# Three pairs of column offsets, in turns, for the weight tiles of a decoder layer

## The chip, the cores and the metric

The kernel runs on one core of one Trainium2 chip. The metric is the device time of one execution in microseconds (us). TensorE (PE) multiplies: it loads a stationary block (LDWEIGHTS, shown as PEld) and streams moving columns past it. VectorE (DVE) and ScalarE (ACT) do elementwise work, GpSimd (POOL) a little of it, and SyncE (SP) issues most of the DMAs.

## The reference

One decoder layer on 256 tokens of width 1024, in float32. With 256 tokens there is one block of attention keys, so the attention is plain causal attention with eight heads.

```python
u = rms_norm(x, attn_pre_norm)
proj = u @ w_in                      # q, k, v, x_lru, g_lru, gate_attn, gate_lru
attn = moba_attention(partial_rope(q), partial_rope(k), v)
y_attn = attn @ w_branch_attn
xc = causal_depthwise_conv(x_lru, conv_w, conv_b)
hl = rg_lru(xc, w_rg_a, b_rg_a, w_rg_i, b_rg_i, lru_lambda)
y_lru = (hl * gelu(g_lru)) @ w_branch_lru
h = x + rms_norm((sigmoid(gate_attn) * y_attn + sigmoid(gate_lru) * y_lru) @ w_out, attn_post_norm)
m = square(relu(rms_norm(h, mlp_pre_norm) @ w_mlp_up)) @ w_mlp_down
out = h + rms_norm(m, mlp_post_norm)
```

## The kernel before

All weights come as 74 chunks of 128 partitions x 2048 float32 (1 MB each), in the order in which they are used. A product in float32 is made of three in the faster 32-bit type float32r: weights and activations are each split into a rounded part `hi` and a remainder `lo`, and `three` (lines 179 to 182) adds hi x hi, hi x lo and lo x hi into the same PSUM bank. `load` brings a chunk into one of three `wraw` buffers by a DMA on SP's queue. `split` (from line 102) writes `hi` on ScalarE (line 117; on VectorE for chunks 17 to 22, line 115) and `lo` on VectorE (line 118). `ahead` keeps four chunks loaded and two split ahead of the one in use.

The tiles `whi` and `wlo` have three buffers each, of 2048 + 64 columns of 4 bytes; `weight_tiles` (lines 96 to 100) takes 2048 columns of each, beginning at the column that the table `OFFSET` (line 45) gives for the chunk, 0 where it has no entry. All six buffers begin at multiples of 64 bytes, as the other large tiles do. The buffers are taken in turns, so up to chunk 39 the remainder of the chunk's number by 3 names the buffer; chunks 40 and 41 have tiles of their own, and from 42 on the turn is shifted by one.

The table names 48 chunks, those whose weights are the stationary operand: chunk 0 (`first_chunk`), 2, 4, 6, 8 to 15 (queries and keys), 16 and 17 (the two gates of the recurrence, lines 336 to 352), 18 to 29 (gates and GeLU branch), 30 to 37 (the two branch projections) and 44 to 57 (MLP up). Each is 48 matmuls of 256 columns (the tokens), for two blocks of 128 output features and eight blocks of input features; the order is `hi` with xh, `hi` with xl, `lo` with xh, so TensorE loads 48 stationary blocks of 128 x 128 per chunk, `hi` twice in a row and then `lo`. In the other chunks (values, output projection, the first two of MLP up, MLP down from 58 on) the weights are the moving operand, 512 columns at a time, and begin at column 0.

Between the feature chunks 18 to 29 stands an attention step each: for some heads the scores (lines 387 and 388), for others the transposes of the probabilities (line 405) and their product with the values (lines 411 and 412), all of them 32-bit matmuls in two passes. The last three steps have no scores left. Chunks 8 to 18 follow each other with nothing between them on TensorE, and so do 30 to 37 and 45 to 57. Ahead of 45 stand four transposes (line 613), ahead of 44 matmuls of 512 columns (lines 602 to 604).

The tile names in the rows: `xgh`, `xgl` are the two parts of the normalised input, `ath`, `atl`, `lrh`, `lrl` those of the branches, `u` both parts of the MLP's input, `rrh`, `rrl` those of its hidden layer.

Of the kernel before, what the change touches and what calls it, by code (L numbers as in the profile page):

```python
# [41 lines left out]

OFFSET = {c: (48, 16) for c in (*range(0, 8, 2), *range(8, 38), *range(44, 58))}


@with_exitstack
def hybrid_layer(ctx: ExitStack, tc: tile.TileContext, head_d, x_d, w_d, cst_d, gp_d, out_d):
# [45 lines left out]
    def weight_tiles(c):  # L95
        hi = whi_p.tile([P, 2048 + W_STEP], F32R, tag="whi", name=f"whi{c}")
        lo = wlo_p.tile([P, 2048 + W_STEP], F32R, tag="wlo", name=f"wlo{c}")
        h, l = OFFSET.get(c, (0, 0))
        return hi[:, h:h + 2048], lo[:, l:l + 2048]
# [637 lines left out]
```

## Time and profile before

| what | value |
|---|---|
| median of three runs | 442.46 us (442.3 to 617.95) |
| the profiled execution | 443.12 us, span 441.3 us |
| TensorE matmuls busy | 429.0 us, 97% |
| VectorE busy | 293.1 us, 66% |
| ScalarE busy | 239.7 us, 54% |
| granted TensorE clock, mean | 0.996 |
| DMA, mean | 189 GB/s |

The span goes from the first to the last instruction; 1.8 us of the execution lie around it. Matmuls overlap each other in the profile, and their ends are modelled, so a busy share near 100% says that TensorE always has something under way, and not at which rate; the rate is read from the starts.

### The profile page before, as it was taken

Reading aid. Unit: us, or ns where it says so; the run is one execution under the profiler, and the core shown is the slowest. Engines: PE = TensorE matmul, PEld = TensorE weight load, DVE = VectorE, ACT = ScalarE, POOL = GpSimd, SP = SyncE. Lnnn points to the kernel's source line nnn. Section 1 sums busy time; section 2 is a strip of 40 time slices with the busy share of each in tenths; the row PEclk is TensorE's granted clock in tenths of the full one; section 3 lists DMA queues with packets and bytes.
Section 4 is the critical chain, followed back from the end, with each engine's and each line's share of the span. In section 5 each row is a group of like instructions: output and inputs, shape, how many; then the busy total and the mean of one; then the engine's idle time right before and its main releaser. Section 6 shows DMA issues by size and latency. Waiting matters only on the chain.

```text
span 441.3 us, 7246 instructions
## 1 busy us (share of the span) xinstructions
PE 429.0 (97%) x3044; PEld 402.0 (91%) x3044; DVE 293.1 (66%) x353; ACT 239.7 (54%) x326; POOL 20.7 (5%) x48
## 2 busy tenths in 40 slices
PE   6989999999999999999999999999999999999994
PEld 6979999999999999999998879999999988888883
DVE  6749975779997666985688665666666644444424
ACT  7595753419977667553455566555555533333321
POOL 1000063202000000000000000000000000000000
PEclk9999999999999999999999999999999999999998
DMA  8968456655543455445567504555554555555202
GB/s 276 409 238 338 176 215 212 222 209 214 193 165 123 161 218 195 166 140 187 186 257 301 197 0 179 174 182 175 175 181 183 192 190 190 192 196 192 83 1 95
DMA packets 14576, 83.61 MB, mean 189 GB/s; under 512 B 1808, under 2 KB 2576, under 8 KB 5456
## 3 DMA queue, kind: packets, MB, share of 16 engines
q1 hardware_dynamic: 13520, 80.39, 50.7%
q0 software_dynamic: 736, 2.36, 1.6%
q8 instruction: 24, 0.39, 0.4%
q10 hardware_dynamic: 288, 0.39, 0.2%
q14 instruction: 8, 0.07, 0.0%
HBM read 81.04 MB, written 1.05 MB: 186 GB/s over the span
## 4 chain that ended last, share of the span: by engine, by line
PE 91%; DMA 5%; ACT 1%; DVE 1%; issue 0%; SPq 0%; DVEq 0%
PE mm L181 19%; PE mm L180 19%; PE mm L182 18%; PE acc L497 8%; PE acc L495 8%; PE acc L496 8%; DMA x_tok<-in_x_dram 2%; DMA wraw<-in_w_dram 1%; DMA xw_a<-in_head_dram 1%; PE up L604 1%; PE up L602 1%; PE v L233 1%; PE up L603 1%; PE v L234 1%; PE rg L181 1%; PE v L235 1%
## 5 line engine op out<-in xcount | busy, mean ns | idle before, releaser
L118 DVE TENSOR_TENSOR wlo<-wraw,whi 128x2048 fp32r<-128x2048 f32 (+2 forms) x78 | 163.6, 2099 | 88.3 <-ACT whi L117 87.9
L117 ACT CAST whi<-wraw 128x2048 fp32r<-128x2048 f32 (+2 forms) x72 | 125.2, 1739 | 95.8 <-PE acc L497 47.1
L180 PE MATMUL mm<-xgh,whi 128*128 128x256 f32 x384 | 107.7, 284 | 4.2 <-ACT xgh L171 4.2
L182 PE MATMUL mm<-xgh,wlo 128*128 128x256 f32 x384 | 106.6, 278 | 1.6 <-DVE wlo L118 1.6
L181 PE MATMUL mm<-xgl,whi 128*128 128x256 f32 x384 | 107.1, 280 | 0.0
L180 PEld LDWEIGHTS mm<-xgh,whi 128*128 128x128 f32 x384 | 72.2, 190 | 4.5 <-ACT xgh L171 4.2
L182 PEld LDWEIGHTS mm<-xgh,wlo 128*128 128x128 f32 x384 | 72.8, 189 | 1.8 <-DVE wlo L118 1.8
L181 PEld LDWEIGHTS mm<-xgl,whi 128*128 128x128 f32 x384 | 72.8, 189 | 0.5
L181 PE MATMUL mm<-u,whi 128*128 128x256 f32 x224 | 63.3, 283 | 0.0
L180 PE MATMUL mm<-u,whi 128*128 128x256 f32 x224 | 62.5, 279 | 0.0
L182 PE MATMUL mm<-u,wlo 128*128 128x256 f32 x224 | 62.4, 278 | 0.0
L497 PE MATMUL acc<-whi,rrl 128*128 128x512 f32 x128 | 49.8, 389 | 0.0
L496 PE MATMUL acc<-wlo,rrh 128*128 128x512 f32 x128 | 49.8, 389 | 0.0
L495 PE MATMUL acc<-whi,rrh 128*128 128x512 f32 x128 | 49.8, 389 | 0.0
L180 PEld LDWEIGHTS mm<-u,whi 128*128 128x128 f32 x224 | 42.1, 188 | 0.0
L182 PEld LDWEIGHTS mm<-u,wlo 128*128 128x128 f32 x224 | 42.0, 188 | 0.0
L181 PEld LDWEIGHTS mm<-u,whi 128*128 128x128 f32 x224 | 41.9, 187 | 0.0
L497 PEld LDWEIGHTS acc<-whi,rrl 128*128 128x128 f32 x128 | 24.0, 188 | 5.0
L496 PEld LDWEIGHTS acc<-wlo,rrh 128*128 128x128 f32 x128 | 24.0, 188 | 5.0
L495 PEld LDWEIGHTS acc<-whi,rrh 128*128 128x128 f32 x128 | 24.0, 188 | 4.9
L637 ACT CAST rrh<-rv 128x512 fp32r<-128x512 f32 x14 | 8.7, 621 | 34.6 <-DVE rv L636 34.6
L181 PE MATMUL mm<-atl,whi 128*128 128x256 f32 x64 | 18.1, 283 | 0.0
(197 smaller groups left out, 667.8 us busy)
## 6 DMA issues: line engine op xcount, KB each, us to landing
wraw<-in_w_dram SPq DMA_DIRECT2D x70, 1024.0 KB, 4.8
wraw<-in_w_dram SPq DMA_DIRECT2D x8, 256.0 KB, 6.1
xw_a<-in_head_dram SPq DMA_DIRECT2D x4, 256.0 KB, 4.3
wraw<-in_w_dram SPq DMA_DIRECT2D x2, 512.0 KB, 7.2
x_tok<-in_x_dram SPq DMA_DIRECT2D x1, 1024.0 KB, 10.5
gp<-in_gp_dram POOLq DMA_DIRECT2D x1, 1024.0 KB, 5.5
xw_b<-in_head_dram SPq DMA_DIRECT2D x3, 256.0 KB, 5.1
out_dram<-res ACTq DMA_DIRECT2D x2, 192.0 KB, 2.0
```

Of the source, the lines that this page charges most:

```text
L117: nc.scalar.copy(hi[:, k:(i + 1) * n], raw[:, k:(i + 1) * n])
L118: nc.vector.tensor_tensor(lo[:, s], raw[:, s], hi[:, s].bitcast(F32), ALU.subtract)
L180: nc.tensor.matmul(out, wh, xh, start=start, stop=False)
L181: nc.tensor.matmul(out, wh, xl, start=False, stop=False)
L182: nc.tensor.matmul(out, wl, xh, start=False, stop=stop)
L233: nc.tensor.matmul(banks[b], xgh[:, kb, s], hi[:, k, :], start=kb == 0, stop=False)
L234: nc.tensor.matmul(banks[b], xgh[:, kb, s], lo[:, k, :], start=False, stop=False)
L235: nc.tensor.matmul(banks[b], xgl[:, kb, s], hi[:, k, :], start=False, stop=kb == KB - 1)
L495: nc.tensor.matmul(out, xh[:, s], hi[:, hs], start=first, stop=False)
L496: nc.tensor.matmul(out, xh[:, s], lo[:, hs], start=False, stop=False)
L497: nc.tensor.matmul(out, xl[:, s], hi[:, hs], start=False, stop=last)
L637: nc.scalar.copy(hi, v)
```

## The change

The table of offsets has the same 48 chunks as before. Each had its `hi` tile begin at column 48 and its `lo` tile at column 16 of its buffer (192 and 64 bytes). Now the remainder of the chunk's number by 3 picks one of three pairs: 13 and 16 columns (52 and 64 bytes), 16 and 13, or 13 and 13.

```diff
-OFFSET = {c: (48, 16) for c in (*range(0, 8, 2), *range(8, 38), *range(44, 58))}
+OFFSET = {c: ((13, 16), (16, 13), (13, 13))[c % 3] for c in (*range(0, 8, 2), *range(8, 38), *range(44, 58))}
```

Sizes, buffers, the instructions of every engine and their order stay as they are; only the places differ from which `hi` and `lo` are read and to which they are written. The first pair has 17 of the 48 chunks, the second 15, the third 16.

## Rows read from the trace of the kernel before

**Rows 1.** The page's first line and its busy times (engine, us, share, instructions)

```profile
span 441.3 us, 7246 instructions
...
PE 429.0 (97%) x3044; PEld 402.0 (91%) x3044; DVE 293.1 (66%) x353; ACT 239.7 (54%) x326; POOL 20.7 (5%) x48
```

**Rows 2.** The page's chain that ended last, shares by engine, then by line

```profile
PE 91%; DMA 5%; ACT 1%; DVE 1%; issue 0%; SPq 0%; DVEq 0%
PE mm L181 19%; PE mm L180 19%; PE mm L182 18%; PE acc L497 8%; PE acc L495 8%; PE acc L496 8%; DMA x_tok<-in_x_dram 2%; DMA wraw<-in_w_dram 1%; DMA xw_a<-in_head_dram 1%; PE up L604 1%; PE up L602 1%; PE v L233 1%; PE up L603 1%; PE v L234 1%; PE rg L181 1%; PE v L235 1%
```

**Rows 3.** The page's costliest groups: busy us, mean ns of one, idle before

```profile
L180 PE MATMUL mm<-xgh,whi 128*128 128x256 f32 x384 | 107.7, 284 | 4.2 <-ACT xgh L171 4.2
...
L180 PEld LDWEIGHTS mm<-xgh,whi 128*128 128x128 f32 x384 | 72.2, 190 | 4.5 <-ACT xgh L171 4.2
```

**Rows 4.** Three stretches of feature chunks: us, engine busy (x instructions), clock, DMA

```profile
core 0: us, PE busy (x) PEld busy (x) DVE busy (x) ACT busy (x) POOL busy (x), PEclk, DMA share, GB/s
53.00:111.00 58.00, 58.00 (x514) 58.00 (x513) 44.90 (x44) 30.38 (x41) 18.11 (x38) 1.00 0.61 217
187.00:231.00 44.00, 44.00 (x373) 44.00 (x372) 32.04 (x28) 21.13 (x17) 0.00 (x0) 1.00 0.55 192
274.00:347.00 73.00, 73.00 (x617) 73.00 (x616) 46.55 (x39) 38.34 (x40) 0.00 (x0) 1.00 0.53 186
```

**Rows 5.** Windows of 3.6 us in chunks 19, 21, 22, 26, 27, 30, 44, 45

```profile
core 0: us, PE busy (x), PEclk, DMA share, GB/s
114.35:117.95 3.60, 3.60 (x34) 1.00 0.71 255
...
126.94:130.54 3.60, 3.60 (x32) 1.00 0.32 66
134.22:137.82 3.60, 3.60 (x34) 1.00 0.00 0
...
162.65:166.25 3.60, 3.60 (x34) 1.00 0.79 298
169.14:172.74 3.60, 3.60 (x32) 1.00 0.08 32
...
187.89:191.49 3.60, 3.60 (x32) 1.00 0.15 48
269.18:272.78 3.60, 3.60 (x34) 1.00 0.69 230
275.13:278.73 3.60, 3.60 (x32) 1.00 0.56 157
```

**Rows 6.** Timeline of TensorE (start, us, what), 512-column matmuls of the down projection

```profile
379.82 0.39 PE L496 MATMUL acc<-wlo,rrh 128*128 128x512 f32 x1
...
381.18 0.39 PE L496 MATMUL acc<-wlo,rrh 128*128 128x512 f32 x1
```

**Rows 7.** Timeline of TensorE, 32-bit matmuls of an attention step

```profile
124.23 0.49 PE L405 MATMUL pT<-ident,pr 128*128 128x128 f32 x3
124.56 0.39 PE L387 MATMUL s<-kT,qT 128*128 128x128 f32 x2
```

**Rows 8.** Groups by shape, then single lines: duration ns min/median/max

```profile
L118 DVE TENSOR_TENSOR wlo<-wraw,whi 128x2048 fp32r<-128x2048 f32 x68 | 155.7, 2290 | 86.2 <-ACT whi L117 86.1
...
L115 DVE CAST whi<-wraw 128x2048 fp32r<-128x2048 f32 x6 | 7.3, 1222 | 2.8 <-PE mm L181 2.6
...
L277 DVE SCALAR_TENSOR_TENSOR xc<-xlp,head,xc x24: 476/478/485, 33.7 to 57.8; 128x256 f32<-128x256 f32 x24
...
L272 DVE TENSOR_TENSOR xlp<-mm,rstd x3: 681/684/685, 40.5 to 48.7; 128x512 f32<-128x512 f32 x3
...
L325 DVE TENSOR_TENSOR qT<-mm,rstd x4: 682/692/692, 58.2 to 74.2; 128x512 f32<-128x512 f32 x4
```

**Rows 9.** Waits of TensorE: for whom, us in total, times, longest

```profile
PE mm L180 <- ACT xgh L171: 4.2, 1, 4.2
PE mm L182 <- DVE wlo L118: 1.6, 1, 1.6
```

## The prediction

> **What bounds the kernel now.** I read the page's busy shares first. TensorE's matmuls are busy for 429.0 of 441.3 us, VectorE for 293.1 and ScalarE for 239.7 [rows 1]. The chain of work that ended last says the same: 91% of it is TensorE, and the three lines of `three`, 180 to 182, hold 19 + 19 + 18 points of that [rows 2]. The view of waits of TensorE names two waits of 4.2 and 1.6 us for other engines and no more [rows 9]. So the time is a sum of distances from one matmul to the next, and a change of the operands' places counts only if it changes those distances (or makes VectorE or ScalarE so slow that TensorE has to wait).
>
> The duration of one matmul in the page (284 ns) is no distance: matmuls overlap, and so does the load of stationary data (190 ns) [rows 3]. The distance comes from a window without a break: matmuls counted in it, divided into the window plus one duration of 0.28 us, since the count takes in those still running at its left edge. From 53 to 111 us (chunks 8 to 18, the end of 18 left out) that is 58.28/514 = 113.4 ns; from 187 to 231 us (chunks 30 to 37) 44.28/373 = 118.7 ns; from 274 to 347 us (chunks 45 to 57) 73.28/617 = 118.8 ns [rows 4]. The granted clock is 1.00 in all three, the upper of its two levels, the instructions are the same, and no engine is waited for. So the same 48 matmuls of a feature chunk run in one of **two states**, which I call close and wide by their distances. They differ by 5.35 ns a matmul, 48 x 5.35 = 0.257 us a chunk.
>
> Which chunk is in which state is seen from equal windows of 3.6 us inside the chunks: 34 matmuls in the close state, 32 in the wide one [rows 5]. Of the 48 feature chunks (the two gate chunks counted in), chunk 0 runs piecewise behind its loads; close are 2, 4, 6, 8 to 20, 22 to 26 and 44, which makes 22; wide are 21, 27 to 37 and 45 to 57, 25 in all. The state is kept from chunk to chunk as long as nothing stands between them, and is chosen anew behind other matmuls: behind an attention step (chunks 19 to 30) or the transposes (chunk 45). Chunks 21 and 24 use the same weight buffers and the same moving tiles, and are in the wide and in the close state. So in this kernel the places alone do not decide the state; how the stream is entered does too.
>
> **The change, part by part.** No instruction is added, removed or moved on any engine; the bytes are the same. What changes is where a chunk's two weight tiles begin: 192 and 64 bytes into the buffer before, now 52 and 64, 64 and 52, or 52 and 52. Three things can follow.
>
> *The writes.* ScalarE writes `hi`, VectorE writes `lo` (2290 ns for one) and for chunks 17 to 22 `hi` too (1222 ns) [rows 8]. No row shows a write that begins off a multiple of 16 bytes. The nearest ones: reads of `xlp` at 1, 2 and 3 columns take 476 to 485 ns, all three alike, and the write of `xlp` at 4 columns takes 684 ns where the same shape to column 0 takes 692 [rows 8]. So I take nothing. If the double-rate copies of the four chunks with `hi` at 13 fell to 2290 ns, that would be 4 x 1.07 = 4.3 us, and VectorE is idle for 58 - 44.9 = 13.1 us of the busiest stretch [rows 4]. The cover is TensorE's own 5.4 us per chunk against some 44.9/58 x 5.4 = 4.2 us of VectorE; it is gone if a `lo` goes from 2.29 to 3.5 us.
>
> *The length of a load.* Two loads in three now begin 52 bytes into one of the 64-byte steps on which every tile began so far: 17 chunks x 32 + 15 x 16 + 16 x 48 = 1552 of the 2304 loads. No row shows such a load. The one on the grid is bounded by the passes of the 32-bit matmuls: three of `pT` start and give way to the next in 0.33 us, 110 ns each with a load of the same 128 x 128 in each [rows 7]. The close state's 113.4 ns is set by the moving data, since a matmul of twice the columns takes twice as long: six of 512 columns from 379.82 to 381.18 us, 226.7 ns each [rows 6]. That leaves the load a gap of 3.4 ns. The far ends of what a start off the grid costs are a gain (if it breaks the meeting that makes the wide state; that is the next part) and 190 - 113.4 = 77 ns, a load that overlaps nothing [rows 3]. The nearest row is the 110 ns of the same load on the grid, so I take a lengthening that stays within the gap: nothing in the close state, and in the wide one, where something beyond the stream is already on the path, the middle of 0 and 3.4 ns, 1.7 ns. [...]
>
> *The state.* The wide state costs 25 x 0.257 = 6.4 us now, and 22 chunks could still fall into it, 5.7 us. What the trace tells: entries behind scores of attention were close in seven of eight (chunks 19 to 26, 21 the exception), entries behind work without scores were wide in five of five (27, 28, 29, 30, 45), the one behind 512-column matmuls was close (44) [rows 5]. Two entries carry most of the wide time: chunk 30 hands its state on to 37 (8 chunks) and chunk 45 to 57 (13 chunks). I take the wide state for a meeting in time of the two streams that TensorE reads, and a start 52 bytes in shifts one against the other; so I expect entries to be drawn again, not all to one side. The likeliest single outcome is that one of the two long stretches turns to the close state: 10.5 chunks on average, -2.7 us. About 15 chunks remain wide, 15 x 48 x 1552/2304 = 485 loads off the grid at 1.7 ns, +0.8 us. Supply does not hold a gain back: the close stretch was fed at 217 GB/s, the long wide ones draw 192 and 186 [rows 4].
>
> **Sum.** -2.7 + 0.8 = -1.9 us. The profiled execution took 443.12 us (span 441.3, 1.8 around it), 0.66 over the median of 442.46; from the median, 440.6 us.
>
> **The rivals.**
> - *The offsets do not matter.* If TensorE's two reads do not meet, nothing changes: 442.5 us. For it: equal places gave both states. Against it: something makes equal instructions 5.35 ns longer while no engine is waited for. [...]
> - *The wide state goes.* A start off the grid keeps the reads from meeting in step: -6.4 us, 436.1 us. Against it: a third of the loads stays on the grid.
> - *Wide everywhere.* Both tiles now begin at nearly the same place of their grid, so what sets one wide sets the other wide: +5.7 us and 1552 loads at 0 to 3.4 ns, 448.1 to 453.4, 450.8 in the middle.
> - *The load off the grid becomes the bound*, the one that ends clearly on the other side. Every one of 1552 matmuls behind such a load waits for it. It passes 2% (8.9 us) when the load is 5.7 ns longer than the stream; at 10 ns it gives 458.0 us, at the 77 ns of a load that hides nowhere 562.0. For it: only 3.4 ns of gap. Against it: the load reads the same 512 bytes, and the reads at odd columns on VectorE cost nothing [rows 8].
> - *The stream itself gets quicker*, to the 110 ns of [rows 7]: 2304 x 3.4 = 7.8 us and the 6.4, 428.3 us. Against it: the same ratio holds for 512 columns, whose places are not touched.
>
> **How the numbers follow.** Forecast 0.42, its own range 437.5 to 444; no effect 0.15; wide state gone 0.15; wide everywhere 0.10; load as bound 0.13; quicker stream 0.05. A measurement of this kernel tells about 2% from no change, that is 433.6 and 451.3. Faster: 0.05. Slower: 0.13 and half of wide everywhere, 0.18. The rest, 0.77, is the same. The range goes from below the case without the wide state, 434.5, to 451.5, just past the middle of wide everywhere, which leaves out about 2 in 10.
>
> **What would show it.** The same windows: 53 to 111 us should again hold about 514 matmuls (a count near 490 means wide everywhere, less than that a load as the bound). The stretches of chunks 30 to 37 and 45 to 57 tell which state each is in, by 113.4 or 118.8 ns. Chunks of the three pairs can be told apart in turn: if the load matters, chunks whose number leaves 2 (both tiles off the grid) are slower than their neighbours by an equal amount everywhere. `lo` and the double-rate `hi` should keep 2290 and 1222 ns. I am wrong if a third distance appears, or if TensorE waits for a weight tile in the middle of the kernel.

## The result, and the profile after

The changed kernel takes 437.88 us (median of 437.08 to 438.56), 4.5 us less than the 442.38 us of before; the ratio to the runs of before is 0.9895, 95% interval 0.988 to 0.991. One execution of the kernel before took 617.95 us, a slow one, and without it that median would be 442.30. The change is faster, by about 1%, which is less than the 2% that the prediction takes as the border of "the same". The time lies in the range that the prediction states, and the gain is 2.4 times the 1.9 us that was forecast.

The page of the changed kernel, its first line and its busy times, to be held against [rows 1]:

```profile
span 436.8 us, 7246 instructions
...
PE 424.4 (97%) x3044; PEld 397.6 (91%) x3044; DVE 292.4 (67%) x353; ACT 238.5 (55%) x326; POOL 21.0 (5%) x48
```

The span is 4.5 us shorter, TensorE's busy time 4.6 us; the other engines did the same work. TensorE's waits for others are the two of [rows 9], word for word. The groups by shape show that the writes cost what they cost in [rows 8] (columns: busy us, mean ns of one, idle before and for whom):

```profile
L118 DVE TENSOR_TENSOR wlo<-wraw,whi 128x2048 fp32r<-128x2048 f32 x68 | 155.8, 2291 | 82.4 <-ACT whi L117 82.3
L117 ACT CAST whi<-wraw 128x2048 fp32r<-128x2048 f32 x62 | 118.3, 1908 | 88.5 <-PE acc L497 46.2 <-PE mm L181 32.3 <-issue 7.5
...
L115 DVE CAST whi<-wraw 128x2048 fp32r<-128x2048 f32 x6 | 7.3, 1224 | 2.7 <-PE mm L181 2.6
```

ScalarE's line before was this:

```profile
L117 ACT CAST whi<-wraw 128x2048 fp32r<-128x2048 f32 x62 | 118.1, 1905 | 93.6 <-PE acc L497 47.1 <-PE mm L181 38.8 <-issue 5.1
```

So the time has to be in the distances. Three windows stand for the three stretches with nothing between their chunks: 58 us in chunks 8 to 18, 42 us in 30 to 37, 68 us in 45 to 57 (the first 2.5 us of 45 left out). The distance is, as in the prediction, the window plus 0.28 us, divided by the matmuls in it. Before (columns: window, its length, TensorE busy and matmuls, clock, DMA share, GB/s):

```profile
52.70:110.70 58.00, 58.00 (x514) 1.00 0.61 217
186.70:228.70 42.00, 42.00 (x355) 1.00 0.53 189
275.80:343.80 68.00, 68.00 (x575) 1.00 0.52 183
```

The changed kernel:

```profile
53.20:111.20 58.00, 58.00 (x510) 1.00 0.61 215
187.30:229.30 42.00, 42.00 (x373) 1.00 0.55 198
274.70:342.70 68.00, 68.00 (x602) 1.00 0.52 186
```

Both long wide stretches are close: 42.28/373 = 113.4 ns where 119.1 stood, 68.28/602 = 113.4 where 118.7 stood. One matmul more or less in a window moves such a distance by 0.2 to 0.3 ns. The early stretch lost four matmuls. The windows of 3.6 us inside single chunks tell where (34 matmuls are the close state; compare [rows 5]); here chunks 2, 8, 9, 10, 28, 30, 44 and 45 of the changed kernel:

```profile
18.84:22.44 3.60, 3.60 (x32) 1.00 1.04 422
...
54.47:58.07 3.60, 3.60 (x32) 1.00 0.47 196
60.20:63.80 3.60, 3.60 (x33) 1.00 0.34 141
65.82:69.42 3.60, 3.60 (x34) 1.00 0.38 157
...
176.78:180.38 3.60, 3.60 (x33) 1.00 0.41 118
...
188.50:192.10 3.60, 3.60 (x34) 1.00 0.22 84
267.78:271.38 3.60, 3.60 (x32) 1.00 0.58 225
273.96:277.56 3.60, 3.60 (x34) 1.00 0.32 96
```

Seven chunks are wide: 2, 8 and 44 (pair 13 and 13) with 32, and 6, 9, 21 and 28 with 33. Chunk 8 is entered wide, 9 still is, 10 is not. Before, 2, 6, 8, 9 and 44 were close and 25 others wide; of those 25, 21 and 28 alone are left, and 23 became close. With the distances that the uniform runs below show, 119.9 ns for 13 and 13 and 117.7 for the others, the seven cost 3 x 48 x 6.5 + 4 x 48 x 4.3 ns = 0.9 + 0.8 = 1.8 us. Taken from the 6.4 us of the 25 that leaves 4.6 us, and the span is 4.5 us shorter. The whole change is accounted for by the distances.

The two long stretches are close from their first chunk on. The prediction counts chunk 30 as an entry, but nothing stands on TensorE between 29 and 30; in the kernel before the last matmul of 29 and the first of 30 are:

```profile
186.05 0.28 PE L182 MATMUL mm<-xgh,wlo 128*128 128x256 f32 x1
186.16 0.28 PE L180 MATMUL mm<-ath,whi 128*128 128x256 f32 x1
```

So the stretch runs from 29 to 37 and is entered at 29, behind an attention step. A window inside 29, before and then after, shows that it was entered wide and is now entered close:

```profile
182.18:185.78 3.60, 3.60 (x32) 1.00 0.24 36
```

```profile
183.06:186.66 3.60, 3.60 (x34) 1.00 0.19 25
```

The state is not there at once: 29 has 6 uneven distances before it is close, and 45 has 16, of 114 to 122 ns, inside the chunk and so with one pair. Neither stretch was thrown out of the wide state by a change of the pair. The one place where the changed kernel loses a steady wide state with nothing in between is from chunk 9 to 10. In no profiled run does a close chunk turn wide with nothing in between.

### The profile page after: what moved, and what is told of

Its sections match the earlier page's. It is cut to its first block, busy times and chain, and to the rows that moved or that the text cites. A ratio compares the mean times of both kernels' runs of the same rounds, so it can differ in the third digit from the quotient of the medians.

```text
span 436.8 us, 7246 instructions
## 1 busy us (share of the span) xinstructions
PE 424.4 (97%) x3044; PEld 397.6 (91%) x3044; DVE 292.4 (67%) x353; ACT 238.5 (55%) x326; POOL 21.0 (5%) x48
## 4 chain that ended last, share of the span: by engine, by line
PE 91%; DMA 5%; ACT 1%; DVE 1%; issue 0%; SPq 0%; DVEq 0%
PE mm L182 18%; PE mm L180 18%; PE mm L181 18%; PE acc L497 8%; PE acc L496 8%; PE acc L495 8%; DMA x_tok<-in_x_dram 3%; DMA wraw<-in_w_dram 1%; DMA xw_a<-in_head_dram 1%; PE up L602 1%; PE up L604 1%; PE rg L182 1%; PE v L234 1%; PE v L233 1%; PE up L603 1%; PE v L235 1%
## 5 line engine op out<-in xcount | busy, mean ns | idle before, releaser
L180 PE MATMUL mm<-u,whi 128*128 128x256 f32 x224 | 62.0, 277 | 0.0
L181 PE MATMUL mm<-u,whi 128*128 128x256 f32 x224 | 62.0, 277 | 0.0
L182 PE MATMUL mm<-lrh,wlo 128*128 128x256 f32 x64 | 17.7, 276 | 0.0
```

The lines of the kernel that those rows point to most:

```text
L180: nc.tensor.matmul(out, wh, xh, start=start, stop=False)
L181: nc.tensor.matmul(out, wh, xl, start=False, stop=False)
L182: nc.tensor.matmul(out, wl, xh, start=False, stop=stop)
```

## The experiments

Two theories were open after this. *Turns*: a steady wide state lives only as long as the stationary tiles keep their place from chunk to chunk, and the change of the pair ends it. *Off the grid*: a tile that begins 52 bytes in, off the 64-byte steps, cannot stay in the wide state. A third, *one pair*, gives all credit to 16 and 13, the pair of chunk 10.

All results in one table; the distances are those of the three windows, in ns, each from the profiled execution; times are medians. The kernel before, timed beside them, took 442.45 us in the first group of four (1 to 4), 442.61 in the second (5 to 8) and 442.46 in the third (9 to 11).

| run | 8 to 18 | 30 to 37 | 45 to 57 | us | ratio, 95% interval |
|---|---|---|---|---|---|
| before | 113.4 | 119.1 | 118.7 | 442.38 | |
| the change | 114.3 | 113.4 | 113.4 | 437.88 | 0.9895, 0.988 to 0.991 |
| 1: 13, 13 everywhere | 119.9 | 113.4 | 113.4 | 440.39 | 0.996, 0.9933 to 0.9987 |
| 2: 13, 16 everywhere | 117.7 | 117.8 | 113.4 | 440.83 | 0.9971, 0.9947 to 0.9995 |
| 3: 16, 13 everywhere | 117.7 | 117.8 | 113.4 | 441.89 | 0.9978, 0.9951 to 1.0005 |
| 4: 16, 16 everywhere | 117.7 | 113.4 | 117.9 | 442.82 | 1.0001, 0.9986 to 1.0016 |
| 5: three pairs on the grid, in turns | 114.3 | 113.4 | 113.6 | 436.80 | 0.9862, 0.9841 to 0.9884 |
| 6: the pairs from 27 on alone | 113.4 | 113.4 | 113.2 | 436.20 | 0.9865, 0.9832 to 0.9898 |
| 7: transposes ahead of 57 | 113.2 | 119.1 | 113.6 | 439.15 | 0.9915, 0.9893 to 0.9936 |
| 8: two pairs, by entry | 113.2 | 113.4 | 113.2 | 436.24 | 0.986, 0.9837 to 0.9882 |
| 9: all tiles 64 bytes on | 113.2 | 119.1 | 113.2 | 442.12 | 0.9986, 0.9966 to 1.0005 |
| 10: weights 64 bytes back | 118.2 | 118.4 | 118.3 | 446.51 | 1.0094, 1.0064 to 1.0123 |
| 11: the others 64 bytes on | 118.2 | 118.1 | 118.3 | 447.91 | 1.0125, 1.004 to 1.0211 |

### One pair everywhere (runs 1 to 4)

The diff of run 1; in runs 2, 3 and 4 the pair is (13, 16), (16, 13) and (16, 16).

```diff
-OFFSET = {c: (48, 16) for c in (*range(0, 8, 2), *range(8, 38), *range(44, 58))}
+OFFSET = {c: (13, 13) for c in (*range(0, 8, 2), *range(8, 38), *range(44, 58))}
```

> All 48 chunks take the third pair, 13 and 13. In the changed kernel single chunks with it (2, 8, 44) ran at a steady 120.0 ns a matmul, and 8 lost the wide state two chunks later, in a chunk with 16 and 13. Theory 'turns' (a wide state stays as long as the geometry stays; the change of the pair from chunk to chunk throws it out): chunks 8 to 18, with nothing between them, all stay at 120.0 ns, 9 more chunks x 0.32 us over the changed kernel, and a stretch entered wide keeps it, so 441 us or more. Theory 'off the grid' (a load that begins 52 bytes in cannot stay in step): 113.4 ns from chunk 9 or 10 on, about 437 us.

> All 48 chunks take the first pair, 13 and 16. In the changed kernel chunks 6, 9 and 21 ran at 117.8 ns with it. 'Turns': chunks 8 to 18, if entered wide, stay at 117.8 ns, 9 more chunks x 0.21 us, and the same for 30 to 37 and 45 to 57 where they are entered wide: 440 to 445 us. 'Off the grid': 113.4 ns in all long stretches, about 437 us.

> All 48 chunks take the second pair, 16 and 13. In the changed kernel this pair ended wide stretches (chunks 4, 10, 19, 22, 25) and stayed wide once (28, 117.8 ns). Theory 'one pair' (16 and 13 alone does the work): nearly all chunks at 113.4 ns, 436 to 437 us. 'Turns': the stretch from 28 stays wide up to 37 and others are drawn by their entry, 438 to 443 us.

> All 48 chunks take 16 and 16, both on the 64-byte steps but at the same place as each other. 'Off the grid': wide stretches as in the kernel before, some 20 chunks or more at 118 to 120 ns, 441 to 448 us. 'Turns': the same, since nothing changes from chunk to chunk. If instead it is the distance between the two weight tiles and the moving tile that counts and not the grid, all stretches may be at 113.4 ns, 436 us.

The windows of run 1 (13 and 13):

```profile
52.40:110.40 58.00, 58.00 (x486) 1.00 0.59 201
189.20:231.20 42.00, 42.00 (x373) 1.00 0.58 202
276.50:344.50 68.00, 68.00 (x602) 1.00 0.52 186
```

486 matmuls are 119.9 ns over the whole of chunks 8 to 18. In the changed kernel the wide state that this pair gives chunk 8 was gone by chunk 10. The other two stretches are close, with every load off the grid. Run 3 (16 and 13):

```profile
51.80:109.80 58.00, 58.00 (x495) 1.00 0.60 209
189.00:231.00 42.00, 42.00 (x359) 1.00 0.53 193
277.90:345.90 68.00, 68.00 (x602) 1.00 0.52 187
```

It is wide in the first two, so *one pair* falls: 16 and 13 is no cure by itself. Run 4, with both tiles on the grid, has the wide distance of runs 2 and 3 (495 matmuls, 117.7 ns):

```profile
52.20:110.20 58.00, 58.00 (x495) 1.00 0.60 208
189.10:231.10 42.00, 42.00 (x373) 1.00 0.54 198
276.30:344.30 68.00, 68.00 (x579) 1.00 0.53 186
```

All four keep the wide state from 8 to 18 once it is there, off the grid or on it, as *turns* has it and *off the grid* does not. The size of the gain was missed: run 1 came in at 440.4 where *turns* said 441 or more, since its late entries came out close. Each pair also picks its own entries: 45 is entered close with a 13 in the pair, wide without (run 9 has an exception); 29, and 30 to 37 with it, is entered close with 13 and 13 and with 16 and 16, wide with the other two and with 48 and 16; 8 is entered wide with all four and close with 48 and 16. The changed kernel has 13 and 13 at chunk 29 and 13 and 16 at 45. Run 1 has the first at 29 and run 2 the second at 45, without any turn, and both entries are close there too. So the close state of the two long stretches comes from the pair at the entry. In the changed kernel the turn is needed for 8 to 18 alone.

### Turns without a 13 (run 5)

```diff
+OFFSET = {c: ((48, 16), (16, 48), (16, 16))[c % 3] for c in (*range(0, 8, 2), *range(8, 38), *range(44, 58))}
```

> Three pairs in turns, all on the 64-byte steps: 48 and 16, 16 and 48, 16 and 16. Theory 'turns' (the change of geometry from chunk to chunk ends a wide stretch, wherever the tiles begin): 30 to 37 and 45 to 57 close except for a chunk or two behind an entry, as in the changed kernel; some 436 to 439 us. Theory 'off the grid and turns' (a pair with 13 has to be among them): wide stretches of many chunks stay, 441 to 443 us.

Three pairs on the 64-byte steps, taken in turns, give 436.8 us. Chunks 8, 9, 10, then 44, 45 and 46 in windows of 3.6 us:

```profile
52.87:56.47 3.60, 3.60 (x33) 1.00 0.61 255
58.54:62.14 3.60, 3.60 (x32) 1.00 0.50 203
64.18:67.78 3.60, 3.60 (x34) 1.00 0.35 146
...
266.13:269.73 3.60, 3.60 (x33) 1.00 0.66 225
272.24:275.84 3.60, 3.60 (x32) 1.00 0.34 109
277.91:281.51 3.60, 3.60 (x34) 1.00 0.21 82
```

8 and 9 are wide, and 10 is close. 44 is wide, 45 behind the transposes is entered wide too, as with 48 and 16 everywhere, and 46 is close where the kernel before stays wide up to 57. *Off the grid* falls here: no 13 is needed to end a wide stretch, a turn does it. Not every change of the pair did: the one from 8 to 9 left the state wide both here and in the changed kernel, and all three ends (10 twice, 46) come at a chunk whose number leaves 1. Whether other changes would end it is not shown.

### Where the gain sits (run 6)

```diff
+OFFSET = {c: ((13, 16), (16, 13), (13, 13))[c % 3] if 27 <= c < 38 or c >= 45 else (48, 16) for c in (*range(0, 8, 2), *range(8, 38), *range(44, 58))}
```

> The changed kernel's three pairs in chunks 27 to 37 and 45 to 57 alone; 0 to 26 and 44 keep 48 and 16. 'Turns': the whole gain sits in the two long stretches, and the early chunks, which the change made wide (2, 6, 8, 9, 44), are close again: 0.0053 x 48 x 24 chunks = 6.4 us less than the kernel before, less some 0.4 us of chunks behind entries, 436.4 us, faster than the changed kernel by 1.4. If the early chunks' places help the later ones in some way: 438 us or more.

436.2 us against 436.4 expected, and by the medians 1.7 below the change, though the two intervals of the ratio overlap. The distances say it more clearly: 113.4 ns in 8 to 18 where the change has 114.3, and the long stretches as in the change. The pairs are worth all they bring in 27 to 37 and 45 to 57; in the early chunks they did harm, since entries that 48 and 16 had passed close became wide.

### The entry alone (run 7)

```diff
...
-    t1 = up_tokens(1)
+    t1 = up_tokens(1, slot_tile(0, "upt1", F32, (P, 512)))
...
-        if j == 0:
+        if j == 12:
             up_transposed(1, t1)
```

> Offsets of the kernel before everywhere; only the four transposes that stand ahead of chunk 45 are moved ahead of chunk 57 (their input in a tile of its own). Theory 'entry' (the state is chosen where a stretch is entered and kept): 44 is close, so 45 to 56 are close as well, 12 x 0.266 = 3.2 us less, 439.3 us; 57 may be wide. Theory 'place' (these tiles at these places drift into the wide state by themselves): 45 to 56 wide, 442.4 us.

No offset is changed; the four transposes move, and their input has a tile of its own. Chunks 44, 45, 46, 56 and 57:

```profile
268.52:272.12 3.60, 3.60 (x34) 1.00 0.73 216
273.96:277.56 3.60, 3.60 (x34) 1.00 0.43 182
279.40:283.00 3.60, 3.60 (x34) 1.00 0.36 148
333.80:337.40 3.60, 3.60 (x34) 1.00 0.39 164
339.75:343.35 3.60, 3.60 (x32) 1.00 0.40 130
```

45 to 56 take over the close state of 44, and 57, now behind the transposes, is wide. 439.15 us against 439.3 expected, and all four executions lie between 439.0 and 439.3. The kernel before took 442.61 beside it, 3.5 us more, and 12 chunks x 0.257 us are 3.1 of them: the very same weight tiles at the same places run sooner because nothing breaks the stream ahead of them.

### A pair for each kind of entry (run 8)

```diff
+OFFSET = {c: (48, 16) if c < 19 or c == 44 else (13, 13) for c in (*range(0, 8, 2), *range(8, 38), *range(44, 58))}
```

> Chunks 0 to 18 and 44 with 48 and 16, the others with 13 and 13: for every kind of entry the pair that came out close in the runs so far (behind 512-column matmuls 48 and 16, behind attention steps and transposes 13 and 13). If entry and geometry together choose the state and it is then kept: no wide chunk at all, 6.5 us of distances over 113.33 ns in the kernel before fall to some 0.5, so 436.4 us. If the pair ahead of an entry matters too, one of the long stretches is wide again: 438 to 440 us.

Its page and its three windows:

```profile
span 433.8 us, 7246 instructions
```

```profile
51.50:109.50 58.00, 58.00 (x515) 1.00 0.62 218
184.80:226.80 42.00, 42.00 (x373) 1.00 0.55 199
271.80:339.80 68.00, 68.00 (x603) 1.00 0.53 188
```

436.24 us, 6.4 less than before, and close in all three. There is no turn from 19 to 37 or from 45 to 57 here, and both long stretches are close, entered with 13 and 13. With run 6 (436.20) it has the lowest median, 1.6 us under the change; runs 5, 6 and 8 can't be told apart by their intervals.

### Distance or place (runs 9 to 11)

Run 9 has the first edit (all tiles behind the first few 64 bytes on), run 10 the second (weight tiles 64 bytes back), run 11 both.

```diff
-GAPS = {"const": 1, "s5": 4}
+GAPS = {"const": 3, "s5": 4}
-OFFSET = {c: (48, 16) for c in (*range(0, 8, 2), *range(8, 38), *range(44, 58))}
+OFFSET = {c: (32, 0) for c in (*range(0, 8, 2), *range(8, 38), *range(44, 58))}
```

> Offsets of the kernel before; every tile of the kernel but the first few begins 64 bytes later (a longer gap at the start of the memory). Theory 'distance' (what counts is how the stationary and the moving tiles stand to each other): the same chunks wide as in the kernel before, 21, 27 to 37 and 45 to 57 at 118.9 ns, 442.4 us. Theory 'absolute place' (a certain address of a weight tile makes a load slow): other chunks are wide, or another distance than 118.9 ns.

> Both weight tiles begin 16 columns (64 bytes) earlier than in the kernel before, 32 and 0; the moving tiles stay. 'Distance': another set of wide chunks or another distance than before, and the same set as in the run in which the other tiles are moved 64 bytes forward under the same weights. 'Absolute place': a set that differs from that run's.

> The weight tiles stand at the addresses of the kernel before (offsets 32 and 0 behind a gap that is 64 bytes longer); all the other tiles, the moving ones among them, begin 64 bytes later. 'Distance': the set of wide chunks of the run with 32 and 0 alone, chunk for chunk. 'Absolute place of the weights': the set of the kernel before, 21, 27 to 37 and 45 to 57.

Run 10, then run 11:

```profile
51.90:109.90 58.00, 58.00 (x493) 1.00 0.58 207
190.00:232.00 42.00, 42.00 (x357) 1.00 0.52 189
279.20:347.20 68.00, 68.00 (x577) 1.00 0.51 184
```

```profile
55.30:113.30 58.00, 58.00 (x493) 1.00 0.59 206
193.40:235.40 42.00, 42.00 (x358) 1.00 0.53 193
282.60:350.60 68.00, 68.00 (x577) 1.00 0.51 183
```

No chunk is close in either, and the counts agree to one matmul, though every address of the one is 64 bytes from that of the other. Run 11 has its weights exactly where the kernel before has them, whose counts were 514, 355 and 575. So the distance between the weight tiles and the other tiles decides, and not the place of the weights. All the other tiles move together here; that the moving operands are the ones that count is a reading, since every matmul of the trace has one beside its weights (`mm<-xgh,whi`). (Run 11's windows begin 3.4 us later: in that execution TensorE waited 1.9 us longer in chunk 4 and then ran 15 matmuls at some 213 ns, at a granted clock of 0.59 from 31 to 34 us; over the whole execution the clock is 0.993 against 0.997 in run 10. That is its whole difference from run 10, a span of 447.7 against 444.4 us; its other execution took 446.3 us.)

Run 9 keeps all distances and has the wide chunks of the kernel before up to 37. Its last stretch was close in the profiled execution, which took 438.9 us:

```profile
51.90:109.90 58.00, 58.00 (x515) 1.00 0.62 218
185.90:227.90 42.00, 42.00 (x355) 1.00 0.53 190
275.00:343.00 68.00, 68.00 (x603) 1.00 0.53 188
```

The second stretch counts 355 as before, the third 603 where 575 stood. Of its ten executions two took 438.9 and eight 442.0 to 442.6, a gap of 3.3 us, and 13 chunks x 0.257 us are 3.3 us. Only one of the two kinds was profiled, so that the other eight had 45 to 57 wide is worked out from the times.

## Why the prediction was wrong in size and right in sign

- **What bounds the kernel** held. TensorE is the chain, the gain is in the distances between matmuls, and 4.6 us of them add up to the 4.5 us of the span. (Of the two levels of the granted clock in the trace of before, the lower is 0.50; it stands from 438 us on, behind the last matmul.)
- **The writes** cost nothing, as taken: 2291 and 1224 ns against 2290 and 1222 [rows 8], and 1908 against 1905 on ScalarE.
- **The length of a load** costs nothing in the close state, as taken: run 1 has all loads 52 bytes in and 42.28/373 = 113.4 ns, the close distance. (The transposes `pT` of [rows 7], from which the 110 ns on the grid were read, have one pass each and loads of 140 ns, not 190; the two passes of `s` from 124.56 to 124.78 us, with loads of 190 ns, give the same 110: 220 ns for 128 columns of plain float32, where 256 columns of float32r take 113.4.) The 1.7 ns in the wide state was the wrong idea, and no run shows it: 13 and 16, 16 and 13, and 16 and 16 (no load off the grid) are all at 117.7 ns, below the 118.7 to 119.1 of before, and 13 and 13 is at 119.9. The wide distance goes with the pair and not with the number of loads off the grid. For the seven wide chunks it comes to 1.8 us, what seven at the old distance would have cost, so the +0.8 us was not there.
- **The state** is the term that failed: -2.7 us forecast, -4.6 by the distances. The step was "one of the two long stretches turns to the close state", 10.5 chunks, with about 15 left wide. Both turned. Of the 25 wide chunks 23 became close, worth 23 x 0.257 = 5.9 us; 2, 6, 8, 9 and 44, close before, came out wide and took back 1.3 (0.9 for the three with 13 and 13, 0.4 for the two others). I took an entry for a draw. At 8, 29, 44 and 45 its outcome goes with the pair that the chunk there has, in every profiled run but run 9 (chunk 45): 13 and 13 closes 29, and 13 and 16 closes 45, in turns or not (runs 1, 2 and 8). It is no rule for every entry: with 16 and 13, chunks 19, 22 and 25 are close in the changed kernel and wide in the trace of run 3. The rows of before, with one pair everywhere, could not tell which pair closes which entry, so the forecast's right sign is in part luck.
- **The state is kept** "from chunk to chunk as long as nothing stands between them" is a second step that failed, in the stretch where I forecast no change. It is a rule of the kernel before, in which every chunk has the same two places; I carried it over to a kernel in which they change with every chunk. There the close state is kept, and the wide one is not. Chunk 8 came out wide, which I had not counted on: I had looked for new outcomes at attention steps and transposes alone. By the rule 8 to 18 would then all be wide, at 117.7 to 119.9 ns as in runs 1 to 4, and the change would have lost some 1.7 to 2.9 us more. It has 114.3 ns there, wide in 8 and 9 alone. With the entries as they came, the rule would have given a gain of 1.6 to 2.8 us, near the forecast by two errors that cancel.
- **The entries.** Counting 30 as one was a wrong reading: work without scores stood ahead of four wide entries (27, 28, 29, 45), and the first long stretch is the nine chunks from 29 on. What makes a pair close one entry and not another is open.
- **The rivals.** *The wide state goes* (436.1 us) was nearer to the 437.88 us than the forecast, with the wrong reason: run 1, with every load off the grid, is wide from 8 to 18, at 119.9 ns. *The offsets do not matter* is out by 446.5 against 442.5 us in run 10. Runs 10 and 11 differ from the kernel before in nothing but the distance between the weight tiles and the others, and every chunk is wide, at 118.1 to 118.4 ns where 8 to 18 had 113.4; so equal instructions do not have one distance whatever the offsets. *The load as the bound* is out by run 1, with 113.4 ns from 30 to 37, *the quicker stream* by the close stretches, at 113.2 to 113.4 ns in every run. *Wide everywhere* exists, but for another geometry (run 10, 446.5 us).
- "I am wrong if a third distance appears": two appeared in the changed kernel, and the uniform runs put them at 117.7 and 119.9 ns.

Open: that the two reads meet in the memory is my reading of runs 9 to 11, in which another distance between the tiles takes 8 to 18 from 113.2 to 118.2 ns; no row shows a read being held up, nor why the wide state, once entered, stays. Nor is it shown why one program enters chunk 45 in both ways, as run 9 does.

## What to carry to other kernels

Where TensorE is busy without a break, count matmuls in equal windows: the duration of one says little (0.28 us in both states here), and 5% of the rate was lost (118.8 against 113.4 ns) with no wait in any view. If two such rates appear for the same instructions, look at what stands ahead of each stretch, and at where stationary and moving tiles begin; choosing the place by the kind of entry (run 8) and taking it in turns from chunk to chunk, which kept a bad entry from being held (run 5), came out within each other's intervals here. A rule read off a trace (here: the state is kept) holds for what was constant in that trace, so ask whether the change keeps it constant.

## What the runs showed of the hardware

Not expected: the wide state has a distance that belongs to the geometry and came back in the runs that had the geometry: 117.7 to 117.9 ns for 13 and 16, 16 and 13, and 16 and 16, 118.1 to 118.4 for 32 and 0, 118.7 to 119.1 for 48 and 16, 119.9 for 13 and 13, against 113.2 to 113.4 for the close state, which came out with every pair but 32 and 0. And one program can fall to either side of an entry from one execution to the next: run 9 took 438.9 or 442.0 to 442.6 us, though only an execution of the first kind was profiled.
